# A hybrid RWKV-7 and delta-net layer on one core: delta-net decays from broadcast rows of running sums, 32x32 tiles in the heads' inversion, and a new order

## The chip, the cores and the metric

The kernel runs on one core of one Trainium2 chip. The metric is the device time of one execution in microseconds (us). Three runs of the kernel before took 2287.71 to 2296.7 us, median 2291.92 us.

## The reference, cut to what matters

One layer over 256 latent tokens and 256 context tokens, model width 2048, all float32. A projection `w_in` feeds two mixers: a bidirectional RWKV-7 mixer (16 heads of 64) and a bidirectional gated delta-net (8 heads of 128). Their outputs are merged under gates, projected, and a SwiGLU network follows. What the change touches is the delta-net's decay. Per head, direction and chunk of tokens, with g the log-decay of a token:

```
gc = jnp.cumsum(chunks(g), axis=-1)
diff = gc[..., :, None] - gc[..., None, :]
decay = jnp.where(incl, jnp.exp(jnp.where(incl, diff, 0.0)), 0.0)
lmat = jnp.where(strict, jnp.einsum('nbhik,nbhjk->nbhij', kb, kc) * decay, 0.0)
sol = lax.linalg.triangular_solve(lmat, rhs, left_side=True, lower=True, unit_diagonal=True)
qk = jnp.where(incl, jnp.einsum('nbhik,nbhjk->nbhij', qc, kc) * decay, 0.0)
q_dec = qc * jnp.exp(gc)[..., None]
```

The reference uses chunks of 64; the kernel works in blocks of 128 tokens, two latent and two context.

## The kernel before, in words

**Stages.** First come the modulation vectors and the low-rank columns (to about 300 us). Then one long woven stage holds the products with `w_in` and both mixers: eight RWKV pairs (to about 840 us), then eight delta-net heads (840 to about 1290 us). After it come the merge with `pa` and `pb`, `w_out`, the SwiGLU and the output (to 2289 us). Every large product splits float32 weights into a high part (`whi`, cast on ScalarE) and a low part (`wlo`, subtracted on VectorE) and runs three matmuls for each 128x128 tile of weights, into the PSUM tile `mm`.

**What sets the order.** The woven stage is written as generators (`prepare`, `grams`, `inverse`, `scan` per RWKV pair; `features`, `tokens`, `decays`, `head_grams`, `head_inverse`, `head_scan` per delta-net head; `products` and `cast` for the weights; `ada_rest` for the remaining modulation columns). A planner, `Weave`, gives each operation an estimated cost, picks the one that can start first, and breaks ties by a number per kind in `RANK`. The order that comes out is fixed on TensorE (PE), VectorE (DVE), ScalarE (ACT) and GpSimd (POOL), each of which runs its instructions in that order. DMAs that SyncE (SP) issues go in an order that the framework's scheduler sets. `GATES_A` and `GATES_B` say after which pair or head how many of the 40 gate products (fillers with no reader in this stage) become available.

**Decays.** For head h and direction d, `decays(h)` multiplies the column of log-decays by a triangle on DVE (tile `gm`, 128x512), multiplies that on PE by the constant matrix `aft[d]` (128x128 by 512 columns) to get all differences of running sums, takes Exp out of PSUM on ACT into `Ed{d}`, and masks it with the triangle on POOL. A second matmul, of `ones` by the first 256 columns of `gm`, gives the running sum itself, the same on every partition; ACT takes Exp of it into `eq`, and DVE multiplies q by it into `Qe`. `decays(h)` may begin when `head_grams(h-1)` is done; `head_grams(h)` reads `Ed0` and `Ed1`.

**Inversion.** `invert` solves the triangular systems: blocks of 16 go through DRAM (`scr`, `tscr`) and a loop of 15 steps on DVE, and are then joined into 32 and 64 by small matmuls into the PSUM tile `pi`. The RWKV pairs call it with nu=16, the heads with nu=8. In the joining step named in the diff, `Tx` is multiplied by `Qm` in 64x64 tiles, 16 matmuls of 16 columns for nu=8. Head h+1's inversion begins with the transposes `T<-LT` on DVE and the stores `scr<-LT` and `scr<-T` on SP.

**Names in the trace.** Nearly all planned instructions show the one line that records them (L146; L124 and L163 for the DMAs of POOL and SP). Tiles in the shared arena read as `arena`, the constants as `C`, PSUM banks as `pa`, `pi`, `s`, `mm`. So `pa<-arena,C` of 128x512 on PE is the `aft` matmul, or the sum of squares of k in `features`; of 128x256 it is the `ones` matmul, or the sum of squares of q; `arena<-C,gtok` on DVE is the product `gm`; `arena<-arena,C` on POOL is the mask.

Of the kernel before, what the change touches and what calls it, by code (L numbers as in the profile page):

```python
# [11 lines left out]
F32 = mybir.dt.float32  # L12
# [15 lines left out]
GATES_A, GATES_B = (6, 2, 3, 4, 0, 1, 4, 3), (2, 3, 0, 1, 1, 0, 9, 1)  # L28

RANK = dict(cast=-94, lowrank=-64, prepare=53, grams=-6, inverse=-58, values=6, scan=-54, begin=181, head_scan=90, head_inverse=100, head_grams=123, decays=122, tokens=90, features=160, gate_out=137, lowrank_out=99, row_tile=486)  # L30
# [8 lines left out]
for _name, _w in (("ident", 128), ("ones", 128), ("bd64", 128), ("rmask", 256),  # L39
                  ("low16", 2), ("eye16", 32), ("tri", 256), ("aft", 256), ("q4", 4), ("q2", 2),  # L40
                  ("eps", 1), ("gneps", 1)):
    _C[_name] = (_n, _n + _w)
    _n += _w
# [12 lines left out]
def const_array():  # L56
    c = np.zeros((P, NC_COLS), np.float32)

    def put(name, a):
        lo, hi = _C[name]  # L60
        c[:, lo:hi] = np.asarray(a, np.float32).reshape(P, hi - lo)

    i = np.arange(P)
    put("ident", np.eye(P))
    put("ones", np.ones((P, P)))
    put("bd64", (i[:, None] // 64) == (i[None] // 64))
    s, t = (i % 64)[:, None], np.arange(64)[None]
# [8 lines left out]
    put("aft", np.concatenate([u > v, u < v], 1))  # L76
    put("q4", (i[:, None] % 4) == np.arange(4)[None])
# [34 lines left out]
class Lane:  # L112
# [5 lines left out]
    def __getattr__(self, name):  # L118

        def op(out, *a, **k):  # L120
            if name == "preload_act_table_set":
                return Op(self, 1.3, lambda: self.engine.preload_act_table_set(out))
            if name == "dma_start":
                return Op(self, 0.6 if self.each > 0.002 else 0.06, lambda: self.engine.dma_start(out, *a))  # L124
# [153 lines left out]
def emit(ctx: ExitStack, tc, A, out, dbg=None):  # L278
# [7 lines left out]
    g = Lane(G, 0.06, 0.0024, LAT["own"])  # L286
# [29 lines left out]
    aft = c_("aft").rearrange("p (d t) -> p d t", d=2)  # L316
    eps, gneps = c_("eps"), c_("gneps")
# [245 lines left out]
    def invert(pool, Lt, parts, nu, which, full, fill):  # L563
# [63 lines left out]
        yield [e.matmul(pv[64 * h:64 * h + 64, 1, u], Tx[64 * h:64 * h + 64, u, :], Qm[64 * h:64 * h + 64, u, :],  # L627
                        start=True, stop=True) for u in range(nu) for h in range(2)]
# [46 lines left out]
    btok = cst.tile([P, 4, 16], F32, name="btok")  # L675
    egc = cst.tile([P, 4, 16], F32, name="egc")
# [385 lines left out]
    def products():  # L1062
# [24 lines left out]
        while todo or nxt:  # L1087
# [27 lines left out]
            else:  # L1115
# [5 lines left out]
    gplaces = (("kvq", 1280, 2), ("l2s", 512, 1), ("gm", 512, 1), ("Ed0", 512, 1), ("Ed1", 512, 1), ("eq", T, 1), ("ob", 8 * T, 1),  # L1121
# [5 lines left out]
             "VX0": [P, 8, 2, 64], "VX1": [P, 8, 2, 64], "KB": [P, 2, 8, 2, 64], "ivx": [P, 16, 64], "Y": [P, 4, 64], "R1": [P, 2, 64],  # L1127
# [29 lines left out]
    def begin():  # L1157
# [6 lines left out]
        t2 = gs.tile([P, 512], F32, tag="gm", name="t2")[:, 0:P]  # L1164
# [18 lines left out]
        yield v.tensor_scalar(sp, sp, al, -1.0, ALU.mult, ALU.mult)  # L1183
        ps = yield pab
        yield [e.transpose(ps[:, 0:P], sp, ident), e.transpose(ps[:, P:2 * P], bet, ident)]
        yield v.tensor_copy(gtok, ps[:, 0:P].rearrange("p (b c) -> p b c", b=4)[:, :, 0:16])
        yield v.tensor_copy(btok, ps[:, P:2 * P].rearrange("p (b c) -> p b c", b=4)[:, :, 16:32])
# [92 lines left out]
    def decays(h):  # L1280
# [6 lines left out]
        qe = []  # L1287
        for d in range(2):
            col = 8 * d + h
            gm = gs.tile([P, 4, P], F32, tag="gm", name="gm")  # L1290
            yield v.tensor_mul(gm, tri[:, d].unsqueeze(1).to_broadcast([P, 4, P]),
                               gtok[:, :, col:col + 1].to_broadcast([P, 4, P]))
            gf = gm.rearrange("p b c -> p (b c)")
            ps = yield pab
            yield e.matmul(ps, aft[:, d], gf, start=True, stop=True)
            ed = gs.tile([P, 4, P], F32, tag=f"Ed{d}", name="Ed")
            yield s.activation(ed.rearrange("p b c -> p (b c)"), ps, AF.Exp)
            weave.release(pab)
            yield g.tensor_mul(ed, ed, tri[:, d].unsqueeze(1).to_broadcast([P, 4, P]))
            Ed.append(ed)  # L1300
            if d == 0:
                yield "feat", h
                yield "scan", NPAIR - 1 if h else NPAIR - 2
                if h > 1:
                    yield "gscan", h - 2
                o["Qe"] = gs.tile([P, 2, T], F32, tag="Qe", name="Qe")
# [458 lines left out]
```

## Time and profile before

| what | value |
|---|---|
| median of three runs | 2291.92 us |
| the profiled execution's own time | 2291.02 us |
| its span, first to last instruction | 2289.2 us |
| granted TensorE clock, mean | 0.978 |
| busy share of the span: PE, DVE, ACT, POOL | 96%, 68%, 47%, 5% |

The 1.8 us between the profiled time and its span lie outside the instructions. PE's busy time counts pipelined matmuls whose ends are modelled; the distance from one start to the next says what a matmul really costs. `PEld` is the weight load that goes with each matmul.

### The profile page before, as it was taken

What the parts mean: (1) busy time and instruction counts of PE and PEld (TensorE: products, weight loads), DVE (VectorE), ACT (ScalarE), POOL (GpSimd) and SP (SyncE); (2) the same over time, 40 slices, a digit from 0 to 9 for tenths busy, and PEclk for the clock granted to TensorE, in tenths of its full rate; (3) what the DMA queues carried; (4) which work ended last, traced back from release to release, by engine and by line L of the source; (5) the groups of instructions that cost most, each with busy time, mean ns of one, the idle gap of its engine ahead of it and who ended that gap; (6) DMA issues with size and microseconds to landing.
All of it is one profiled execution on the core that took longest, in us unless ns stands there. A gap on an engine that the chain in (4) does not pass through costs nothing. (4 is left out here: it accounts for less than half of the span.)

```text
span 2289.2 us, 53997 instructions
## 1 busy us (share of the span) xinstructions
PE 2191.2 (96%) x22584; PEld 1944.7 (85%) x22584; DVE 1566.3 (68%) x3233; ACT 1068.0 (47%) x1894; POOL 115.2 (5%) x185
## 2 busy tenths in 40 slices
PE   7998999999999999999999989899999999999998
PEld 4766587777878778878889888889999999999997
DVE  3446488778888668888899768774656655545444
ACT  3245555444454455444545464443444444444443
POOL 0000000000000010111101040000000000000000
PEclk9999999989999999999999999999999999999999
DMA  9955544344343436455557777854777776566665
GB/s 388 402 143 166 171 119 131 94 104 108 107 118 107 119 106 190 142 165 157 166 160 251 250 280 266 290 194 144 233 240 235 235 231 213 188 184 192 187 188 162
DMA packets 231924, 430.72 MB, mean 188 GB/s; under 512 B 114944, under 2 KB 129152, under 8 KB 227328
## 3 DMA queue, kind: packets, MB, share of 16 engines
q1 hardware_dynamic: 203744, 350.72, 49.9%
q0 software_dynamic: 14112, 51.39, 7.1%
q10 hardware_dynamic: 13824, 25.17, 3.3%
q8 instruction: 177, 2.90, 0.5%
q14 instruction: 67, 0.55, 0.1%
HBM read 401.44 MB, written 25.77 MB: 187 GB/s over the span
## 5 line engine op out<-in xcount | busy, mean ns | idle before, releaser
L368 DVE TENSOR_TENSOR wlo<-wraw,whi 128x1024 fp32r<-128x1024 f32 x328 | 394.1, 1202 | 329.9 <-ACT whi L367 327.0
L367 ACT CAST whi<-wraw 128x1024 fp32r<-128x1024 f32 x328 | 337.6, 1030 | 478.9 <-PE mm L378 429.2
L146 PE MATMUL mm<-hxh,whi 128*128 128x256 f32 (+1 forms) x1376 | 467.5, 340 | 6.2 <-ACT whi L146 6.0
L146 PE MATMUL mm<-hxh,wlo 128*128 128x256 f32 (+1 forms) x1376 | 465.9, 339 | 4.1 <-DVE wlo L146 3.9
L146 PE MATMUL mm<-hxl,whi 128*128 128x256 f32 (+1 forms) x1376 | 465.7, 338 | 0.0
L379 PE MATMUL mm<-hfh,wlo 128*128 128x256 f32 x1344 | 376.1, 280 | 0.5 <-DVE wlo L368 0.5
L377 PE MATMUL mm<-hfh,whi 128*128 128x256 f32 x1344 | 376.1, 280 | 0.0
L378 PE MATMUL mm<-hfl,whi 128*128 128x256 f32 x1344 | 375.9, 280 | 0.0
L146 PEld LDWEIGHTS mm<-hxh,whi 128*128 128x128 f32 x1376 | 264.3, 192 | 33.9 <-ACT whi L146 7.4
L146 PEld LDWEIGHTS mm<-hxh,wlo 128*128 128x128 f32 x1376 | 264.2, 192 | 31.4 <-DVE wlo L146 6.1
L146 PEld LDWEIGHTS mm<-hxl,whi 128*128 128x128 f32 x1376 | 264.0, 192 | 25.9 <-issue 5.4
L146 DVE TENSOR_TENSOR wlo<-wraw,whi 128x512 fp32r<-128x512 f32 x344 | 236.5, 689 | 68.1 <-ACT whi L146 66.3
L146 ACT CAST whi<-wraw 128x512 fp32r<-128x512 f32 x344 | 205.0, 617 | 112.6 <-PE mm L146 79.0
L379 PEld LDWEIGHTS mm<-hfh,wlo 128*128 128x128 f32 x1344 | 253.2, 188 | 0.9 <-DVE wlo L368 0.9
L377 PEld LDWEIGHTS mm<-hfh,whi 128*128 128x128 f32 x1344 | 253.4, 189 | 0.0
L378 PEld LDWEIGHTS mm<-hfl,whi 128*128 128x128 f32 x1344 | 253.2, 188 | 0.0
L146 DVE TENSOR_TENSOR arena<-arena 128x28 f32<-128x28 f32 (+13 forms) x538 | 133.1, 249 | 23.6 <-DMA arena<-scr 10.5
L377 PE MATMUL mm<-za,whi 128*128 128x256 f32 x512 | 143.3, 280 | 0.0
L379 PE MATMUL mm<-za,wlo 128*128 128x256 f32 x512 | 143.2, 280 | 0.0
L378 PE MATMUL mm<-za,whi 128*128 128x256 f32 x512 | 143.2, 280 | 0.0
L378 PEld LDWEIGHTS mm<-za,whi 128*128 128x128 f32 x512 | 96.4, 188 | 0.0
L379 PEld LDWEIGHTS mm<-za,wlo 128*128 128x128 f32 x512 | 96.4, 188 | 0.0
(320 smaller groups left out, 3978.5 us busy)
## 6 DMA issues: line engine op xcount, KB each, us to landing
wraw<-w SPq DMA_DIRECT2D x172, 512.0 KB, 4.1
wraw<-wgu SPq DMA_DIRECT2D x168, 512.0 KB, 4.4
aw<-ada_rest POOLq DMA_DIRECT2D x96, 512.0 KB, 5.2
aw<-ada_first SPq DMA_DIRECT2D x32, 1024.0 KB, 11.2
wraw<-wdn SPq DMA_DIRECT2D x64, 448.0 KB, 3.7
wraw<-wout SPq DMA_DIRECT2D x32, 512.0 KB, 4.8
aw<-ada_gt ACTq DMA_DIRECT2D x64, 256.0 KB, 4.8
wraw<-wdn SPq DMA_DIRECT2D x32, 512.0 KB, 3.7
```

Source lines behind the costliest of these rows:

```text
L146: return Op(self, cost, lambda: getattr(self.engine, name)(out, *a, **k), kind)
L367: S.copy(hi[:, c, :M], raw[:, c, :M])
L368: V.tensor_sub(lo[:, c, :M], raw[:, c, :M], hi[:, c, :M].bitcast(F32))
L377: E.matmul(ps, hi, Xh[:, k, :n], start=first and i == 0, stop=False)
L378: E.matmul(ps, hi, Xl[:, k, :n], start=False, stop=False)
L379: E.matmul(ps, lo, Xh[:, k, :n], start=False, stop=last and i == len(wt) - 1)
```

## The change

Four things change together.

1. `begin` makes the running sums once: after the log-decays `sp` it adds two scans of 128x128 on DVE (forward and backward), stores their rows to a DRAM tile `grow` with eight small DMAs, and transposes them on PE along with the two transposes that were there, so that `gct` holds the sums by token.
2. `decays` has no matmul left. Per direction, one DMA reads a row of 512 sums from `grow` into all 128 partitions (`row`, one buffer); POOL subtracts `gct` from it; DVE takes the minimum with a new constant `past` (0 inside the triangle, -200 outside); ACT takes Exp. The Exp for `Qe` reads `row` itself, into `eq` for d=0 and in place for d=1. The wait for `features`, the scan and `gscan` moves behind both directions.
3. For nu=8 the step of `invert` becomes 32 matmuls in 32x32 tiles instead of 16 in 64x64.
4. Numbers that set the order: eight entries of `RANK`, `GATES_B`, and, in the planner, its two cost figures for POOL and the threshold by which it knows a DMA issued on POOL. The constants grow by 256 columns for `past`.

```diff
-GATES_A, GATES_B = (6, 2, 3, 4, 0, 1, 4, 3), (2, 3, 0, 1, 1, 0, 9, 1)
+GATES_A, GATES_B = (6, 2, 3, 4, 0, 1, 4, 3), (2, 2, 0, 1, 0, 1, 10, 1)
...
-    g = Lane(G, 0.06, 0.0024, LAT["own"])
+    g = Lane(G, 0.17, 0.0019, LAT["own"])
...
+        if nu == 16:
+            yield [e.matmul(pv[64 * h:64 * h + 64, 1, u], Tx[64 * h:64 * h + 64, u, :], Qm[64 * h:64 * h + 64, u, :],
+                            start=True, stop=True) for u in range(nu) for h in range(2)]
+        else:
+            yield [e.matmul(pv[r, 1, u], Tx[r, u, b:b + 32], Qm[r, u, :], start=True, stop=True) for h, u, b, r in fours]
...
+        yield v.tensor_tensor_scan(t0, ones, sp, 0.0, ALU.mult, ALU.add)
+        yield v.tensor_tensor_scan(t1[:, ::-1], ones, sp[:, ::-1], 0.0, ALU.mult, ALU.add)
+        for d, t in enumerate((t0, t1)):
+            for b in range(4):
+                dq(grow[d, :, P * b:P * b + P], t[32 * b:32 * b + 16])
...
-            gm = gs.tile([P, 4, P], F32, tag="gm", name="gm")
-            yield v.tensor_mul(gm, tri[:, d].unsqueeze(1).to_broadcast([P, 4, P]),
-                               gtok[:, :, col:col + 1].to_broadcast([P, 4, P]))
-            gf = gm.rearrange("p b c -> p (b c)")
-            ps = yield pab
-            yield e.matmul(ps, aft[:, d], gf, start=True, stop=True)
+            row = gs.tile([P, 4, P], F32, tag="row", name="row")
+            yield dq(row.rearrange("p b t -> p (b t)"), grow[d, 8 * d + h, :].partition_broadcast(P))
             ed = gs.tile([P, 4, P], F32, tag=f"Ed{d}", name="Ed")
-            yield s.activation(ed.rearrange("p b c -> p (b c)"), ps, AF.Exp)
-            weave.release(pab)
-            yield g.tensor_mul(ed, ed, tri[:, d].unsqueeze(1).to_broadcast([P, 4, P]))
+            yield g.tensor_sub(ed, row, gct[:, :, col:col + 1].to_broadcast([P, 4, P]))
+            yield v.tensor_tensor(ed, ed, past[:, d].unsqueeze(1).to_broadcast([P, 4, P]), ALU.min)
+            yield s.activation(ed.rearrange("p b c -> p (b c)"), ed.rearrange("p b c -> p (b c)"), AF.Exp)
             Ed.append(ed)
             if d == 0:
...
-            ps = yield pab
-            yield e.matmul(ps[:, :T], ones, gf[:, 0:T], start=True, stop=True)
-            eq = gs.tile([P, T], F32, tag="eq", name="eq")
-            yield s.activation(eq, ps[:, :T], AF.Exp)
-            weave.release(pab)
-            yield v.tensor_mul(o["Qe"][:, d], o["q"], eq)
+                first = gs.tile([P, T], F32, tag="eq", name="eq")
+                yield s.activation(first, row[:, 0:2].rearrange("p b c -> p (b c)"), AF.Exp)
+        yield "feat", h
+        yield "scan", NPAIR - 1 if h else NPAIR - 2
+        if h > 1:
+            yield "gscan", h - 2
+        o["Qe"] = gs.tile([P, 2, T], F32, tag="Qe", name="Qe")
+        yield v.tensor_mul(o["Qe"][:, 0], o["q"], first)
+        eq = row[:, 0:2].rearrange("p b c -> p (b c)")
+        yield s.activation(eq, eq, AF.Exp)
+        yield v.tensor_mul(o["Qe"][:, 1], o["q"], eq)
```

Over the whole program PE loses 16 matmuls of 128x512 and 16 of 128x256 and 128 of 64x16, and gains 256 of 32x16 and two transposes; DVE trades 16 products for 16 minima and gains two scans and two small copies; ACT's 32 Exps read SBUF instead of PSUM; POOL trades 16 products for 16 subtractions; SP gains 16 row loads and eight small stores.

PE in the middle of the delta-net stage, where the matmuls of one head's `w_in` columns (`mm`) run between the two steps `s<-TF,keg` that open a head's scan. Before:

```order
L146 MATMUL s<-TF_10240,keg 128x128 x4
L146 MATMUL mm<-hxh,wlo 128x512
L146 MATMUL mm<-hxh,whi 128x256
L146 MATMUL pa<-arena,C 128x512
L146 MATMUL s<-TF_10240,keg 128x128 x4
L146 MATMUL mm<-hxl,whi 128x256
```

The same step of a head after the change:

```order
L147 MATMUL mm<-hxl,whi 128x512
L147 MATMUL s<-TF_10136,keg 128x128 x4
L147 MATMUL mm<-hxh,wlo 128x512
L147 MATMUL mm<-hxh,whi 128x512
L147 MATMUL mm<-hxl,whi 128x512
L147 MATMUL mm<-hxh,wlo 128x512
L147 MATMUL mm<-hxh,whi 128x512
L147 MATMUL mm<-hxl,whi 128x512
L147 MATMUL s<-TF_10136,keg 128x128 x4
```

The decay's `aft` matmul is gone from between them; products alone fill the place.

DVE where one head's grams end (`PT`) and the next head's decay and inversion begin (`T<-LT`), with what each row waits for. Before:

```order
L146 TENSOR_TENSOR PT<-pa,arena 128x256
L146 SCALAR_TENSOR_TENSOR aw<-aw,ck 128x512 [waits DMASW4_49,DVE_49]
L146 TENSOR_TENSOR wlo<-wraw,whi 128x512 [waits DMAHW7_49,PE_49,Activation_49]
L146 TENSOR_TENSOR PT<-pa,arena 128x256
L146 SCALAR_TENSOR_TENSOR aw<-aw,ck 128x512 [waits DVE_49]
L146 TENSOR_TENSOR wlo<-wraw,whi 128x512 [waits Activation_49]
L146 COPY arena<-pi 128x256 [waits PE_49]
L146 TENSOR_TENSOR arena<-C,gtok 128x512
L146 SCALAR_TENSOR_TENSOR aw<-aw,ck 128x512 [waits DMASW5_49,DVE_49]
L146 SCALAR_TENSOR_TENSOR aw<-aw,ck 128x512 [waits DVE_49]
L146 STREAM_TRANSPOSE T_12267<-LT 64x256
```

After, the stretch from the minimum of direction 0 to the minimum of direction 1 (`arena<-arena,C`) of one head:

```order
L147 TENSOR_TENSOR arena<-arena,C 128x512 [waits Pool_49]
L147 SCALAR_TENSOR_TENSOR aw<-aw,ck 128x512 [waits DMASW3_49,DVE_49]
L147 SCALAR_TENSOR_TENSOR aw<-aw,ck 128x512 [waits DVE_49]
L147 STREAM_TRANSPOSE T_11582<-LT 64x256
L147 SCALAR_TENSOR_TENSOR aw<-aw,ck 128x512 [waits DMASW4_49,DVE_49]
L147 STREAM_TRANSPOSE T_11582<-LT 64x256
L147 TENSOR_TENSOR wlo<-wraw,whi 128x512 [waits DMAHW1_49,PE_49,Activation_49]
L147 SCALAR_TENSOR_TENSOR arena<-mm,PR,arena 128x2x254 [waits Activation_49]
L147 SCALAR_TENSOR_TENSOR aw<-aw,ck 128x512 [waits DVE_49]
L147 TENSOR_TENSOR wlo<-wraw,whi 128x512 [waits Activation_49]
L147 SCALAR_TENSOR_TENSOR arena<-mm,PR,arena 128x2x255 [waits DVE_49]
L147 TENSOR_TENSOR arena<-arena,C 128x512 [waits Pool_49]
```

The product that waited for nothing has become a minimum that waits for POOL, and ten rows stand between the two minima.

SP at the same head's start, with waits. Before, the stores that open an inversion:

```order
L163 DMA wraw<-w 128x1024 [waits DMAHW5_49,DVE_49]
L163 DMA scr_105<-LT 64x4x64 [waits DMAHW6_49,DVE_49]
L163 DMA scr_105<-LT 64x4x64 [waits DMAHW7_49]
L163 DMA wraw<-w 128x1024 [waits DMAHW2_49,DMAHW0_49,DVE_49]
L163 DMA scr_105<-T_12908 64x4x64 [waits DMAHW1_49,DVE_49]
L163 DMA scr_105<-T_12908 64x4x64 [waits DVE_49]
```

After:

```order
L164 DMA wraw<-w 128x1024 [waits DMAHW3_49,DVE_49]
L164 DMA scr_105<-LT 64x4x64 [waits DMAHW4_49,DVE_49]
L164 DMA scr_105<-LT 64x4x64 [waits DMAHW5_49]
L164 DMA wraw<-w 128x1024 [waits DMAHW6_49,DMAHW0_49,DVE_49]
L164 DMA arena<-grow 128x512 [waits DMAHW7_49,Activation_49,Pool_49]
L164 DMA scr_105<-T_11582 64x4x64 [waits DVE_49]
L164 DMA scr_105<-T_11582 64x4x64 [waits DMAHW1_49,DVE_49]
L164 DMA wraw<-w 128x1024 [waits DMAHW2_49,DVE_49]
```

The row load of direction 1, which waits for ACT and POOL, stands ahead of the stores `scr<-T`.

More of the change, by code (lines that the diff above doesn't have):

```diff
@@ L27 @@
 DECAY = 0.6065306597126334
-GATES_A, GATES_B = (6, 2, 3, 4, 0, 1, 4, 3), (2, 3, 0, 1, 1, 0, 9, 1)
-RANK = dict(cast=-94, lowrank=-64, prepare=53, grams=-6, inverse=-58, values=6, scan=-54, begin=181, head_scan=90, head_inverse=100, head_grams=123, decays=122, tokens=90, features=160, gate_out=137, lowrank_out=99, row_tile=486)
+GATES_A, GATES_B = (6, 2, 3, 4, 0, 1, 4, 3), (2, 2, 0, 1, 0, 1, 10, 1)
+RANK = dict(cast=-94, lowrank=-64, prepare=59, grams=-6, inverse=-56, values=6, scan=-39, begin=181, head_scan=145, head_inverse=100, head_grams=123, decays=122, tokens=77, features=120, gate_out=137, lowrank_out=105, row_tile=486)
 LAT = dict(dma=2.04, hop=0.255, own=0.092, grp=32, cg=4, turn=0.17)
@@ L39 @@
 for _name, _w in (("ident", 128), ("ones", 128), ("bd64", 128), ("rmask", 256),
-                  ("low16", 2), ("eye16", 32), ("tri", 256), ("aft", 256), ("q4", 4), ("q2", 2),
+                  ("low16", 2), ("eye16", 32), ("tri", 256), ("aft", 256), ("past", 256), ("q4", 4), ("q2", 2),
                   ("eps", 1), ("gneps", 1)):
@@ L123, in op @@
             if name == "dma_start":
-                return Op(self, 0.6 if self.each > 0.002 else 0.06, lambda: self.engine.dma_start(out, *a))
+                return Op(self, 0.6 if self.each > 0.0012 else 0.06, lambda: self.engine.dma_start(out, *a))
             n = int(np.prod(out.shape[1:]))
@@ L316, in emit @@
     aft = c_("aft").rearrange("p (d t) -> p d t", d=2)
+    past = c_("past").rearrange("p (d t) -> p d t", d=2)
     eps, gneps = c_("eps"), c_("gneps")
@@ L675, in emit @@
     btok = cst.tile([P, 4, 16], F32, name="btok")
+    gct = cst.tile([P, 4, 16], F32, name="gct")
+    grow = dpool.tile([2, 16, 512], F32, name="grow")
     egc = cst.tile([P, 4, 16], F32, name="egc")
```

24 lines of the change are left out of this document (10 added, 14 removed).

## The prediction, made before the changed kernel ran

> **What bounds the kernel now.** I read the busy times by stage first, then what PE waits for inside the stage that changes, then the rows around the matmuls that go. Busy time by stage; the columns are the stage and its length, PE, PEld, DVE, ACT, POOL, the granted clock, the DMA share and GB/s:
>
> ```profile
> 300.00:840.00 540.00, 525.07 (x7500) 425.35 (x7499) 426.90 (x1053) 276.15 (x639) 16.77 (x42) 0.97 0.41 108
> 840.00:1290.00 450.00, 438.68 (x4246) 377.51 (x4246) 388.55 (x1012) 218.46 (x433) 51.73 (x76) 1.00 0.60 177
> 1290.00:1560.00 270.00, 244.88 (x2060) 235.21 (x2060) 197.75 (x287) 131.61 (x204) 41.85 (x53) 0.95 0.73 251
> 1560.00:2260.00 700.00, 699.48 (x5993) 699.07 (x5992) 385.72 (x502) 303.78 (x374) 0.00 (x0) 1.00 0.68 209
> ```
>
> Delta-net heads run from 840 to 1290 us: PE is busy 438.7 of 450 us, idle 11.3. DVE is second with 388.6, so 61 us are left on it. All that PE waited for there (total, times, longest):
>
> ```profile
> PE pa L146 <- ACT arena L146: 6.0, 7, 1.3
> PE pi L146 <- DVE T L146: 2.7, 2, 1.7
> PE pi L146 <- DVE arena L146: 1.1, 3, 0.6
> PE s L146 <- DVE Vn L146: 0.6, 2, 0.3
> ```
>
> No wait for weights (`whi`, `wlo`) is among them, and none for the decays' products: the 6.0 us stand before the sum of squares in `features`. So **PE's own queue bounds this stage**, and a matmul taken out of it should shorten it by its length, until DVE or a DMA round trip is late instead.
>
> **What goes from PE.** Rows of PE in order of time (start, duration) around an `aft` matmul and a `ones` matmul:
>
> ```profile
> 1169.71 0.28 PE L146 MATMUL mm<-hxh,wlo 128*128 128x256 f32 x1
> 1169.83 1.02 PE L146 MATMUL pa<-arena,C 128*128 128x512 f32 x2
> 1170.29 0.68 PE L146 MATMUL mm<-hxh,whi 128*128 128x256 f32 x1
> 1170.81 0.28 PE L146 MATMUL mm<-hxl,whi 128*128 128x256 f32 x1
> ...
> 1173.19 0.28 PE L146 MATMUL mm<-hxh,wlo 128*128 128x256 f32 x1
> 1173.30 0.59 PE L146 MATMUL pa<-arena,C 128*128 128x256 f32 x2
> 1173.55 0.47 PE L146 MATMUL mm<-hxh,whi 128*128 128x256 f32 x1
> 1173.85 0.28 PE L146 MATMUL mm<-hxl,whi 128*128 128x256 f32 x1
> ```
>
> Products start 0.12 apart (1169.71 to 1169.83). From 1169.71 to 1170.81 are two such steps and the `aft` matmul: 1.10 - 0.24 = 0.86 us. From 1173.19 to 1173.85: 0.66 - 0.24 = 0.42 us. Each happens 16 times: **13.8 and 6.7 us**.
>
> The inversion's step, old form and a burst of the form that replaces it:
>
> ```profile
> 1236.13 1.11 PE L146 MATMUL pi<-arena,Tx 64*64 64x16 f32 x32
> 1237.17 0.39 PE L146 MATMUL mm<-hxh,whi 128*128 128x256 f32 x1
> ```
> ```profile
> 1171.72 0.73 PE L146 MATMUL pi<-T,LT 32*32 32x16 f32 x64
> 1172.37 0.39 PE L146 MATMUL mm<-hxh,wlo 128*128 128x256 f32 x1
> ```
>
> Start to start 1.04 against 0.65 us: 0.39 less, eight times, **3.1 us**. The new burst has the same count of tiles as the other 32x16 step, so I take its time. Two transposes are added:
>
> ```profile
> L146 PE MATMUL pa<-C,arena 128*128 128x128 f32 x226 | 36.2, 277 | 3.8 <-DVE LAc L146 2.9 <-DVE LAl L146 0.9
> ```
>
> 36.2 / 226 = 0.16 each, 0.3 together. PE's queue loses 13.8 + 6.7 + 3.1 - 0.3 = 23.3 us.
>
> **What the other engines trade.** Rows of DVE, POOL and ACT (busy, mean ns):
>
> ```profile
> L146 DVE TENSOR_TENSOR arena<-C,gtok 128x512 f32<-128x512 f32 x16 | 10.7, 672 | 0.0
> L146 DVE TENSOR_TENSOR arena<-arena 128x512 f32<-128x512 f32 x48 | 33.2, 702 | 0.7 <-POOL bon L826 0.3
> ```
> ```profile
> L146 POOL TENSOR_TENSOR arena<-arena,C 128x512 f32<-128x512 f32 x16 | 20.0, 1251 | 237.2 <-ACT arena L146 237.2
> ```
> ```profile
> L146 ACT ACTIVATE arena<-pa 128x512 f32<-128x512 f32 x16 | 9.6, 598 | 12.8 <-PE pa L146 12.8
> L146 ACT ACTIVATE arena<-arena 128x512 f32<-128x512 f32 x56 | 34.2, 629 | 14.5 <-issue 9.6 <-DVE arena L146 4.3
> L146 ACT ACTIVATE arena<-arena 128x256 f32<-128x256 f32 x32 | 13.3, 417 | 14.3 <-DVE arena L146 13.9
> ```
>
> DVE gives up 16 products of 0.67 us and takes 16 minima of the same shape (0.70 by the second row): half a microsecond in all. ACT's Exps differ by some 0.03 us each, POOL's subtraction has the mask's shape and count. DVE's and ACT's spare time hides all this; without cover it would be 16 x (0.03 + 0.06), 1.4 us. The scans, copies and eight stores of `begin` follow its transposes (`gtok`), 79 us ahead of the first grams (`LT`):
>
> ```profile
> 762.51 0.23 DVE L146 COPY gtok<-pa 128x64 f32<-128x64 f32 x1
> ...
> 841.87 0.87 DVE L146 SCALAR_TENSOR_TENSOR LT<-pa,nbtok,arena 128x128 f32<-128x128 f32 x3
> ```
>
> They cost nothing beside RWKV work, and what SP takes to issue them and the 16 rows delays weight loads for which PE never waited. The constants are 128 KB longer, and the start is bound by DMA:
>
> ```profile
> GB/s 388 402 143 166 171 119 131 94 104 108 107 118 107 119 106 190 142 165 157 166 160 251 250 280 266 290 194 144 233 240 235 235 231 213 188 184 192 187 188 162
> ```
>
> 131,072 B at 388 GB/s are **0.3 us**.
>
> **The wait that comes.** There is one `row` buffer, so direction 1's load waits for direction 0's subtraction and for the Exp into `eq`, which on ACT stands behind Exp of `Ed0`, which waits for the minimum of direction 0. From the end of that minimum the path is Exp 0.63, Exp 0.42, the load, subtraction 1.25, then the next minimum. No broadcast row is in the trace; the nearest loads (KB, median us to landing):
>
> ```profile
> arena<-sgd__1342 SPq DMA_DIRECT2D x32, 256.0 KB, 3.6
> ...
> arena<-oad SPq DMA_DIRECT2D x1, 1024.0 KB, 11.5
> ...
> T<-tscr SPq DMA_DIRECT2D x16, 64.0 KB, 2.4
> ...
> arena<-cvec SPq DMA_DIRECT2D x1, 1024.0 KB, 9.3
> ```
>
> Bounds are 2.4 and 11.5. I take 3.6, since `sgd` has this load's shape (128 rows of 2 KB), queue and size. The path is 0.63 + 0.42 + 3.6 + 1.25 = 5.9, and 6.4 with five handovers that I estimate at 0.1 each from this row (the `ones` matmul above ended at 1173.89, its Exp starts 0.05 later):
>
> ```profile
> 1173.94 0.38 ACT L146 ACTIVATE arena<-pa 128x256 f32<-128x256 f32 x1 [1.32 <-PE pa L146]
> ```
>
> The cover is what DVE has between the two minima, the ten rows shown in the change:
>
> ```profile
> L146 DVE SCALAR_TENSOR_TENSOR aw<-aw,ck 128x512 f32<-128x512 f32 x120 | 88.8, 751 | 5.9 <-DMA aw<-ada_rest 5.6
> ...
> L146 DVE STREAM_TRANSPOSE T<-LT 64x256 f32<-64x256 f32 x16 | 7.0, 435 | 0.2
> ```
> ```profile
> L146 DVE TENSOR_TENSOR wlo<-wraw,whi 128x512 fp32r<-128x512 f32 x344 | 236.5, 689 | 68.1 <-ACT whi L146 66.3
> ...
> L146 DVE SCALAR_TENSOR_TENSOR arena<-mm,PR,arena 128x510 f32<-128x510 f32 x32 | 23.6, 736 | 0.1
> ```
>
> Four times 0.75, two times 0.44, 0.69 and 0.74: 6.7 us. Cover and path are level, so I take half a microsecond per head for ACT's queue: **4.0 us**. At 2.4 us nothing is left of it; at 11.5 it is 14.3 - 6.7 = 7.6 per head, 61 us. Behind the waiting minimum on DVE stand `wlo` parts, for which products wait; behind the waiting load on SP stand `scr<-T`, which open the next inversion.
>
> The Trainium skill, DMA: Bandwidth & Descriptors, section Anatomy of one DMA — SWDGE (gpsimd) path, gives a DMA about 2.0 us fixed plus its bytes at 436 GB/s; for 256 KB an estimate by that page is 2.6 us. By it no wait would come, and the sum would be 4 us lower; `sgd`'s 3.6 us is longer than that, and the row is kept.
>
> **The order set anew** moves work among the 11.3 us of PE's idle time; at best it takes the 6.0 and 2.7 us above with it, at worst it adds as much. I take 0.
>
> **The sum**: 23.3 - 0.3 - 4.0 = 19.0 us. From the profiled execution's 2291.0 us (0.9 below the median of the three) this gives **2272 us**.
>
> **Rivals.** For the second one, 50 us of the stage:
>
> ```profile
> 1200.00:1250.00 50.00, 48.96 (x571) 45.85 (x570) 47.34 (x128) 27.87 (x57) 6.31 (x10) 1.00 0.74 225
> ```
>
> *Better* (14%): the load is early enough, and the waits of 6.0 and 2.7 us go too. 2272 - 4 - 9 = 2259. For it: `features` ranks earlier now. Against: the planner had these waits before, too.
> *DVE becomes the bound* (21%): its 388.6 us don't shrink. In a stage of 427 us it would be busy 91% of the time, against 86% now, in a fixed order in which each stall shows. If half of the 23.3 is lost to this, the time is 2280 to 2287, 2283 in the middle. For it: DVE has 2.7 of 50 us left in this row; against: PE waited for DVE 4.4 us in 450.
> *The change doesn't do what it says* (8%): PE was not the limit, and its time turns into waits on the heads' chain of inversions. Only the shorter inversion step is left, 2288. For it: PEld is busy 377.5 of 450 us; against: products start every 0.12 us with no gap. The Trainium skill, Perfetto Trace Analysis, section Identifying the Most-Contended Engine, says that matmul busy time is a bad measure, and that weight-load busy time is the one to use. By it PE has 72 us of room in this stage and the bound would lie elsewhere; the waits of 11 us in all speak against it here.
> *The row load holds up SP* (9%, slower): if a broadcast from DRAM lands as late as `cvec`, the one broadcast in the trace, in 9.3 us, the path is 12.1, and DVE and the stores `scr<-T` wait 5.4 us per head, 43 us in eight heads. Less 23, this is 2291 + 20 = 2311. It turns the sign from a wait of 2.9 us per head (23.3 / 8), a landing of 6.7 us. For it: the path is a loop in series through four queues. Against: `cvec` moves four times the bytes while the DMAs are 73% busy, here 60%. The Trainium skill, DMA: Bandwidth & Descriptors, in the same section, says that a wait is served on the issuing sequencer before dispatch, so that all behind it waits; SP's order makes that matter here.
>
> **How the numbers follow.** My forecast has 48%. The range runs from the better rival, 2259, to 2293, past the rivals without effect; the slower one is left out with 9%, and about as much in tails. A measurement of this kernel can tell about 0.5%, 11.5 us, from no change. Faster by more than that (below 2280.5) takes the forecast, the better rival and a third of the DVE rival: 48 + 14 + 7 = 69%. Within it are the rest of that one and the 8%: 22%. Slower: 9%.
>
> **What would show it.** Right: the head stage ends about 19 us sooner, PE has no `pa<-arena,C` but those of `features`, and PE idle stays under 17 us in it. The load lands in 3 to 4.5 us; DVE's minima wait for POOL under 1 us each. Wrong: DVE waits for POOL of several us before each second minimum, or SP waits before `arena<-grow` with `scr<-T` late; PE waits on `pi` or `wlo` that grow by 10 us or more.

## The result, and the profile after

The changed kernel takes 2268.36 us (median of 11 runs, 2259.78 to 2280.95), the kernel before beside it 2287.64 us (median of 11, 2280.68 to 2296.70). The ratio is 0.9917, 95% interval 0.9894 to 0.9939, which is 14 to 24 us: 19.3 us between the medians, where the prediction had 19.0. The profiled execution took 2273.03 us, its span is 2271.0 us.

The size is right; the way to it is less so. First the stages, cut at the same work in both kernels: the first inversion bursts of RWKV pair 0, of head 0 and of head 7, the FFN's first product, the end. Of the kernel before, then of after (columns: the stretch and its length, PE, PEld, DVE, ACT, POOL, granted clock, DMA share, GB/s):

```profile
259.10:895.50 636.40, 619.18 (x8518) 503.42 (x8517) 501.98 (x1225) 326.00 (x736) 25.14 (x55) 0.97 0.43 115
895.50:1285.10 389.60, 380.87 (x3821) 328.07 (x3821) 338.34 (x892) 188.71 (x378) 43.68 (x64) 1.00 0.59 173
1285.10:1533.60 248.50, 221.10 (x1939) 211.10 (x1938) 187.65 (x263) 124.22 (x189) 42.38 (x54) 0.96 0.80 275
1533.60:2289.20 755.60, 744.24 (x6340) 743.18 (x6340) 411.50 (x546) 319.87 (x402) 0.00 (x0) 0.99 0.64 200
```
```profile
256.80:873.40 616.60, 603.65 (x8441) 489.16 (x8440) 491.12 (x1217) 322.50 (x728) 24.69 (x55) 0.98 0.42 118
873.40:1262.30 388.90, 371.23 (x4031) 323.39 (x4030) 344.22 (x903) 191.33 (x383) 43.38 (x64) 0.99 0.61 184
1262.30:1509.40 247.10, 222.07 (x1999) 212.81 (x1998) 189.82 (x265) 125.84 (x192) 38.93 (x54) 0.97 0.81 279
1509.40:2271.00 761.60, 750.75 (x6340) 749.89 (x6340) 411.55 (x546) 319.67 (x402) 0.00 (x0) 0.99 0.64 199
```

Head 0's inversion comes 22 us sooner (895.5 to 873.4), head 7's 23 us (1285.1 to 1262.3). So in these two executions the lead is there before the heads' first inversion, and between the first and the last of them nothing more is won: 389.6 against 388.9 us. Counted along PE's order with the start-to-start costs of the prediction, some 13 us less of matmuls stand ahead of head 0's inversion (first decays, and products that the new order puts later), some 13 us less between head 0's and head 7's, and 3 us of products more behind it. In the second stretch the 13 us did not become time: PE's idle time there grows from 8.7 us (389.60 - 380.87) to 17.7, and the time at half clock from 3.4 to 10.2 us, which costs 3 more. What PE waited for from 820 to 1270 us of after (total, times, longest):

```profile
PE pa L147 <- ACT arena L147: 6.7, 6, 1.7
PE s L147 <- DVE Vn L147: 4.6, 3, 3.2
PE mm L147 <- ACT whi L147: 1.3, 1, 1.3
PE pi L147 <- issue: 1.2, 1, 1.2
```

The wait of 6.0 before `features` (`pa`) is still there as 6.7, and one on a head's scan (`s<-Vn`, 0.6 before) has come. Behind it stands the wait that the prediction priced. DVE's minima and POOL's subtractions (busy, mean ns, idle time before them), the row loads beside the load from which their landing was taken (KB, median us), and the new burst of 32x32 tiles:

```profile
L147 DVE TENSOR_TENSOR arena<-arena,C 128x512 f32<-128x512 f32 x16 | 11.0, 685 | 8.8 <-POOL arena L147 8.8
L147 POOL TENSOR_TENSOR arena<-arena,gct 128x512 f32<-128x512 f32 x16 | 19.8, 1240 | 151.5 <-DMA arena<-grow 127.2 <-DVE PT L147 24.3
```
```profile
arena<-sgd__1344 SPq DMA_DIRECT2D x32, 256.0 KB, 3.3
...
arena<-grow SPq DMA_DIRECT2D x16, 256.0 KB, 4.0
```
```profile
1207.99 0.73 PE L147 MATMUL pi<-arena,Tx 32*32 32x16 f32 x64
1208.65 0.38 PE L147 MATMUL mm<-hxh,whi 128*128 128x256 f32 x1
```

Durations came out as taken: the minimum 0.685 us (taken 0.70), the subtraction 1.24 (1.25), the burst 0.66 (0.65). The row lands in 4.0 us (median) and not in 3.6, and DVE waits 8.8 us for POOL in eight heads where 4.0 was taken. The loop of one head, from the first minimum over the Exp that frees the row, the load and the subtraction to the second minimum:

```profile
997.10 0.69 DVE L147 TENSOR_TENSOR arena<-arena,C 128x512 f32<-128x512 f32 x1
999.63 0.42 ACT L147 ACTIVATE arena<-arena 128x256 f32<-128x256 f32 x1
1000.11 0.33 SPq L164 DMA_DIRECT2D arena<-grow  x1
1005.04 1.04 POOL L147 TENSOR_TENSOR arena<-arena,gct 128x512 f32<-128x512 f32 x1 [6.91 <-DMA arena<-grow]
1006.12 0.69 DVE L147 TENSOR_TENSOR arena<-arena,C 128x512 f32<-128x512 f32 x1 [1.70 <-POOL arena L147]
```

The load is issued 2.3 us after the end of the first minimum and takes 4.9 to land, and the second minimum starts 8.3 us after that end, 1.7 of them waiting.

In the FFN after lost 6 us (755.6 to 761.6) with the same 6340 matmuls. In 200 us of that stage PE ran 1717 matmuls before and 1701 after:

```profile
2000.00:2200.00 200.00, 200.00 (x1717) 200.00 (x1716) 98.57 (x103) 87.68 (x105) 0.00 (x0) 1.00 0.64 188
```
```profile
2000.00:2200.00 200.00, 200.00 (x1701) 200.00 (x1700) 98.53 (x104) 87.54 (x107) 0.00 (x0) 1.00 0.64 186
```

It is 1% with no clock, wait or DMA to show for it. Eleven of the twelve experiments' profiles have 1716 or 1717 in this stretch, one (e12) has 1701 too, and this execution was 4.7 us above its median, e12's 14.2 above its own. So it looks like a property of single executions and not of the kernel; the cause stays open.

### The profile page after: what moved, and what is told of

The parts are those of the page before. It is cut to its first block, busy times and chain, and to the rows that moved or that the text cites. A ratio compares the mean times of both kernels' runs of the same rounds, so it can differ in the third digit from the quotient of the medians.

```text
span 2271.0 us, 54427 instructions
## 1 busy us (share of the span) xinstructions
PE 2168.7 (95%) x22778; PEld 1931.1 (85%) x22778; DVE 1563.7 (69%) x3237; ACT 1068.6 (47%) x1894; POOL 111.0 (5%) x185
## 4 chain that ended last, share of the span: by engine, by line
PE 66%; DVE 9%; issue 8%; DMA 4%; ACT 2%; POOL 1%; SPq 0%; DVEq 0%; ACTq 0%; POOLq 0%
PE mm L147 17%; PE mm L381 12%; PE mm L380 12%; PE mm L379 12%; PE s L147 5%; PE pa L147 4%; DVE arena L147 3%; PE pi L147 2%; DMA wr<-wgu 1%; DVE wlo L147 1%; DMA aw<-ada_rest 1%; DVE wlo L370 1%; DVE aw L147 1%; ACT arena L147 1%; DVE acc L1540 0%
## 5 line engine op out<-in xcount | busy, mean ns | idle before, releaser
L147 ACT ACTIVATE arena<-arena 128x512 f32<-128x512 f32 (+3 forms) x132 | 76.7, 593 | 49.6 <-DVE arena L147 36.8
```

What stands on the lines that cost most here:

```text
L147: return Op(self, cost, lambda: getattr(self.engine, name)(out, *a, **k), kind)
```

## The experiments

Each ran beside the kernel before. The third and fourth columns split the mean time of a kernel's runs by the granted clock of each run: what is lost to the clock is taken as time x (1 - clock), since in all these traces every stretch that isn't at 1.00 is at 0.50, which costs half its length if PE has work in all of it, and the rest is what is left. The standard error of a mean of the rest is 0.6 to 1.8 us, so that a difference of two is good to some 2 us. Three sets of the kernel before have a rest of 2243.2, 2245.5 and 2245.0 and 41, 42 and 41 us lost.

| kernel | ratio to before, 95% interval | rest, us | lost to the clock, us |
|---|---|---|---|
| after | 0.9917 (0.9894 to 0.9939) | 2228.4 | 40 |
| e1, order alone | 0.9986 (0.9971 to 1.0001) | 2245.3 | 35 |
| e2, 32x32 list alone | 1.0023 (1.0002 to 1.0045) | 2241.7 | 46 |
| e3, after with the old order | 1.0043 (1.0024 to 1.0061) | 2235.2 | 57 |
| e4, decays alone | 0.9958 (0.9935 to 0.9981) | 2227.1 | 48 |
| e11, decays and list in e4's order | 0.9969 (0.9949 to 0.9990) | 2228.8 | 50 |
| e6, after with the old list, same order | 0.9911 (0.9886 to 0.9935) | 2227.3 | 39 |
| e7, 16 matmuls put back | 0.9958 (0.9940 to 0.9977) | 2240.4 | 38 |
| e9, rows loaded twice | 1.0061 (1.0037 to 1.0086) | 2243.5 | 56 |
| e5, two rows | 0.9983 (0.9962 to 1.0004) | 2236.5 | 46 |
| e10, first Exp early | 0.9897 (0.9878 to 0.9917) | 2221.9 | 40 |
| e8, gaps filled | 0.9908 (0.9877 to 0.9939) | 2231.3 | 34 |
| e12, gaps filled, later casts | 0.9890 (0.9869 to 0.9910) | 2231.5 | 31 |

### The parts of the change

**e1_order_alone**: the kernel before with the new numbers (seven entries of `RANK` differ, not eight).

```diff
-RANK = dict(cast=-94, lowrank=-64, prepare=53, ...
+RANK = dict(cast=-94, lowrank=-64, prepare=59, ...
-GATES_A, GATES_B = (6, 2, 3, 4, 0, 1, 4, 3), (2, 3, 0, 1, 1, 0, 9, 1)
+GATES_A, GATES_B = (6, 2, 3, 4, 0, 1, 4, 3), (2, 2, 0, 1, 0, 1, 10, 1)
```

> The kernel before with nothing but the new order: the new RANK and GATES_B, and the planner's two new costs for POOL. TensorE's work is that of before. Theory (the gain is TensorE's shorter queue, the order is worth nothing): within 5 us of before, ratio 0.998 to 1.002. Rival (the gain is the order's): 10 to 20 us faster, ratio 0.991 to 0.996. A third: these numbers were set for the new decays and misplace the old ones, so that the queue waits more: 5 to 20 us slower, ratio 1.002 to 1.009.

0.9986: with the old decays the new numbers are worth some 3 us, by the interval none to 7. The rest is 2 us longer, and 6 us less go to the clock.

**e2_tiles_alone**: the kernel before with the heads' list in 32x32 tiles.

```diff
+        if nu == 16:
...
+        else:
+            yield [e.matmul(pv[r, 1, u], Tx[r, u, b:b + 32], Qm[r, u, :], start=True, stop=True) for h, u, b, r in fours]
```

> The kernel before with nothing but the heads' inversion list in 32x32 tiles (eight lists, one for each head). Theory (TensorE's queue is the bound, and the bursts go from 1.04 to 0.65 us): 3.1 us faster, ratio 0.9986, which an interval of some 0.2% hardly tells from 1. Rival (the burst stands in a chain of waits that other engines set, so its length is hidden): 1.000.

1.0023: neither. The rest falls by 1.5 us, but 5 us more go to the clock. The edit isn't confined to its line: the planner takes another cost and kind for the list, and the order changes in all that comes behind.

**e3_old_order**: the kernel after with the old numbers (the diff of e1, reversed).

> The kernel after with the order undone: the old RANK, GATES_B and planner costs, with the new decays and the 32x32 list kept. Theory (TensorE loses 23.3 us of work, the new waits give 4 back, the order gives nothing): 19 us faster than before, ratio 0.9917, from 0.990 to 0.994. Rival (the order is what gains): 0.997 to 1.001. A third, half by half: 0.994 to 0.997.

1.0043, 29 us behind after (0.0126 of 2287), and no theory had that. By the split 17 us more are lost to the clock and the rest is 7 us longer (the two ran beside different sets of before). Where the heads end, the product with `pa` finds its weights not yet cast (waits of PE from 1290 to 1335 us; after has 0.9 us of this at its own place, from 1262 to 1330):

```profile
PE mm L379 <- ACT whi L369: 8.1, 2, 6.4
```

**e4_decays_alone**: after with the old numbers and the 64x64 list.

> The kernel before with the new decays alone: old order, old 64x64 list. Theory: 13.8 + 6.7 us of matmuls go, 0.3 us of transposes and 0.3 of constants come, new waits take 4: 16 us faster, ratio 0.993, from 0.991 to 0.995. Rival (VectorE bounds the heads' stage, so that at most half of the matmuls' time is gained): 0.996 to 0.998. Against e3_old_order, which has the 32x32 list as well, it shows again what the list is worth: 0.0014 by the theory.

0.9958, 10 us: between the theory's range (to 0.995) and the rival's (from 0.996), and the interval reaches into each. By the split the rest falls by 16.1 us (2243.2 to 2227.1), which is the theory's 16, and 7 us more than before go to the clock; so it takes no bound by DVE to halve the gain, but the times alone don't decide it. In this order DVE waits 3.0 us for POOL, with rows that land in 3.9 us:

```profile
L147 DVE TENSOR_TENSOR arena<-arena,C 128x512 f32<-128x512 f32 x16 | 10.9, 680 | 3.0 <-POOL arena L147 3.0
```

**e11_tiles_in_e4_order**: the 32x32 list in e4's order (the old numbers, and the planner told the old list's cost).

```diff
+            for o in last:
+                o.cost, o.kind = 0.5 * (0.01 + 0.00075 * 16), (64, 64)
```

> The new decays and the 32x32 list in the issue order of the decays alone (the planner is told the cost and kind of the 64x64 list): it differs from e4_decays_alone by the eight lists alone, and from e3_old_order by nothing but what the planner was told. Theory (e3_old_order is slow by its order, and not by the tiles): as e4_decays_alone or up to 3 us faster, ratio to before 0.994 to 0.997. Rival (the 32x32 list itself does harm when it stands in this order): as e3_old_order, 1.003 to 1.006.

0.9969, as e4. So the list does no harm, and e3 is slow by the order that the list's cost led the planner to: e3 and e11 run the same instructions, 0.0074 apart, with intervals that don't meet.

**e6_old_tiles_same_order**: after's order, with 64x64 tiles.

```diff
+            for o in last:
+                o.cost, o.kind = 2 * (0.01 + 0.00037 * 16), (32, 32)
```

> The kernel after with the heads' second inversion list again in 64x64 tiles, while the planner is told the cost and the kind of the 32x32 list: the issue order of all engines stays row for row. Theory (eight bursts of 1.04 in place of 0.65 us on a queue that is the bound): 3 us slower than after, ratio to before 0.993. Rival (the list hides in waits of the stage): as after, 0.9917. If the 32x32 list did harm by itself, as the kernel with it and the old order might suggest: 5 to 15 us faster than after, ratio 0.985 to 0.9895; if that harm came from the order that its cost led the planner to, none of it shows here.

0.9911 against 0.9917. At a fixed order the rest is longer with the new list than with the old one, by 1.1 us here (good to 2) and by 1.7 in e11 against e4 (good to 1.2), where 3.1 less was expected. The rival holds as far as this can tell: the burst is 0.38 us shorter, and no gain from it shows.

The same four runs show what the order is worth with the new decays. e4 and e6 run the same instructions, one in the order drawn with the old numbers and one in after's, and so do e11 and after. The ratio falls by 0.0047 and by 0.0052, 11 and 12 us; the rest is the same within 0.4 us in both pairs, and 9 and 10 us less are lost to the clock.

### Is PE's queue the limit?

**e7_matmuls_back**: two matmuls of constants for each head, ahead of the transposes of v and of k into the same bank, which overwrite them. The rest of the order is after's.

```diff
+            for _ in range(n):
+                E.matmul(ps, ident, C[:, 0:ps.shape[1]], start=True, stop=True)
```

> The kernel after with 16 matmuls of 128x512 of constants put back on TensorE, two for each head, each ahead of the transposes of the tokens into the bank that these overwrite; the planner is not told of them, so that the order of the rest stays. Theory (a matmul in the heads' queue costs its 0.86 us): 13.8 us slower than after, ratio to before 0.9977. Rival (they fall into TensorE's waits, some 19 us in this stage): within 4 us of after, 0.990 to 0.9935. A third, by the clock: work in a wait keeps TensorE from the half clock, so that they cost less than they last, or nothing.

They cost what they should on PE (start to start 0.85 us, 13.6 in all):

```profile
917.50 1.02 PE L570 MATMUL pa<-C 128*128 128x512 f32 x2
918.35 0.60 PE L147 MATMUL pa<-C,arena 128*128 128x128 f32 x4
```

The rest grows by 12.0 us (2228.4 to 2240.4), the lost clock falls by 2, and the ratio rises by 0.0041, 9 us. So most of a matmul's time on PE is time of the kernel here, and PE's queue is the limit; the little that is missing I put down to idle time that the matmuls fill. The 2 us of clock are inside the noise.

### What the new wait costs

**e9_row_twice**: each row is loaded twice.

```diff
+            Q.dma_start(row.rearrange("p b t -> p (b t)"), grow[d, 8 * d + h, :].partition_broadcast(P))
             yield dq(row.rearrange("p b t -> p (b t)"), grow[d, 8 * d + h, :].partition_broadcast(P))
```

> The kernel after with each of the 16 row loads issued twice, the second behind the first's landing, so that a row is there some 4 us later and SP's queue is held by that long; the order of all other rows stays. It prices the rival in which the row load holds up SP and VectorE. If the rows' landing is on the path as that rival had it (turning point 6.7 us, then each microsecond eight times): some 8 us a row, 15 to 40 us slower than after, ratio to before 0.998 to 1.009. Theory (cover by other work of 6.7 us; VectorE's wait grows by 3 to 4 us a head, and TensorE has other work for most of it): 3 to 10 us slower than after, 0.993 to 0.996. If all of it is hidden: 0.9917.

1.0061: 33 us behind after and 14 behind before. Each load lands in 3.8 us, so that the row is whole after some 7.6, past the 6.7 at which the prediction put the turning point. DVE's wait of one head, then the sum of them:

```profile
1081.49 0.48 DVE L147 SCALAR_TENSOR_TENSOR arena<-mm,PR,arena 128x255 f32<-128x255 f32 x1
1086.30 0.69 DVE L147 TENSOR_TENSOR arena<-arena,C 128x512 f32<-128x512 f32 x1 [4.33 <-POOL arena L147]
```
```profile
L147 DVE TENSOR_TENSOR arena<-arena,C 128x512 f32<-128x512 f32 x16 | 11.0, 685 | 36.4 <-POOL arena L147 36.4
```

DVE waits 27.6 us more than in after. The rest grows by 15 us, and 16 more go to the clock: by this split the added waits are paid about twice here.

**e5_two_rows**: a second row buffer (512 columns more); `eq` (256 columns) goes.

```diff
-... ("row", 512, 1), ("Ed0", 512, 1), ("Ed1", 512, 1), ("eq", T, 1), ("ob", 8 * T, 1),
+... ("row", 512, 2), ("Ed0", 512, 1), ("Ed1", 512, 1), ("ob", 8 * T, 1),
...
-                first = gs.tile([P, T], F32, tag="eq", name="eq")
+                first = row[:, 0:2].rearrange("p b c -> p (b c)")
```

> The kernel after with two row buffers: the Exp for Qe of direction 0 goes in place over its row instead of into eq, whose room the second row takes, so that the load for direction 1 no longer waits for that Exp. The order on VectorE, ScalarE and POOL is that of after, and on TensorE's up to the FFN. Theory (the wait of VectorE for direction 1's subtraction, 8.8 us in the run, is all or nearly all on the path): 4 to 9 us faster than after, ratio to before 0.988 to 0.990. Rival (TensorE has other work in that time): as after, 0.9917.

0.9983. DVE's wait for POOL is gone (0.6 us in the run), yet the kernel is slower than after. It doesn't answer the question, as this kernel no longer computes the layer: the second buffer shifts the tiles behind it in the arena by 512 or 256 columns, I take it onto places that other tiles still hold (not traced). Its waits are others, too: PE waits 6.3 us for `Vn` and 4.6 us for `St` at the last heads.

**e10_exp_early**: the Exp that holds the one row buffer goes ahead of Exp of `Ed0`; the planner isn't told.

```diff
+            if d == 0:
+                first = gs.tile([P, T], F32, tag="eq", name="eq")
+                early = s.activation(first, row[:, 0:2].rearrange("p b c -> p (b c)"), AF.Exp)
+                sub.call = lambda a=sub.call, b=early.call: (a(), b())[0]
+                early.call = lambda: None
```

> The kernel after with the Exp of direction 0's row for Qe issued on ScalarE beside POOL's subtraction, ahead of the Exp of Ed, so that the one row buffer comes free some 1.5 us sooner; the planner takes it to be where it was, so the order on TensorE (up to the FFN), VectorE and POOL stays. The wait of VectorE for POOL (8.8 us in the run of after) should fall to 0 to 3 us. Theory (that wait is half on the path): 2 to 6 us faster than after, ratio to before 0.989 to 0.991. Rival (TensorE has other work meanwhile): as after, 0.9917.

0.9897, inside the theory's range: 4.6 us below after by the ratio, 6.5 by the rest (good to 2), at the same lost clock. DVE's minima wait for POOL no more (0.6 us), and the heads' stage (head 0's burst at 870.3, head 7's at 1250.6) takes 380.3 us where after took 388.9; PE idles 13.9 us in it and not 17.7, and the 10.2 us at half clock of that execution of after have no counterpart here:

```profile
L147 DVE TENSOR_TENSOR arena<-arena,C 128x512 f32<-128x512 f32 x16 | 10.9, 679 | 0.6 <-POOL arena L147 0.6
```

So by the middle values half or more of the 8.8 us were on the path; between the theory's 4.4 and all of them the runs don't decide. The intervals of e10 and after overlap, so that the times alone don't exclude the rival; the vanished wait and the shorter stage speak against it.

### The clock

**e8_fill**: 16 matmuls of constants into idle time of PE, ahead of inversion lists of pairs 0, 2, 3 and 6.

```diff
+                                    {0: (0, 4), 2: (6, 0), 3: (0, 4), 6: (0, 2)}.get(p, (0, 0)))
```

> The kernel after with 16 matmuls of 128x256 of constants at four places of the RWKV pairs where TensorE stood idle for 0.8 to 2.9 us and then ran at half clock for 3.4 to 10.2 us: ahead of the inversion's second list in pairs 0 (4), 3 (4) and 6 (2), ahead of its first list in pair 2 (6). They are 6.9 us of matmuls at 0.43, laid into idle time; order and results are those of after. Theory (idle time of a microsecond or two brings the half clock that follows): most of the 27 us at half clock goes, 8 to 13 us faster than after, ratio to before 0.986 to 0.988. Rival (the small matmuls of the inversion bring the half clock, whatever stands before them): as after or up to 4 us slower, 0.9917 to 0.9935.

Pair 2 of after, rows of PE (start, duration, idle time before it) and windows, in which the last three columns are granted clock, DMA share and GB/s:

```profile
414.90 1.27 PE L147 MATMUL pi<-arena 32*32 32x16 f32 x111
419.08 0.32 PE L147 MATMUL pi<-arena 32*32 32x16 f32 x17 [2.91 <-issue]
421.81 2.43 PE L147 MATMUL pi<-arena,Tx 64*64 64x16 f32 x42
```
```profile
416.00:420.00 4.00, 1.09 (x39) 0.67 (x28) 1.25 (x5) 0.00 (x0) 0.00 (x0) 0.94 0.40 154
420.00:424.00 4.00, 4.00 (x47) 3.01 (x46) 1.21 (x2) 2.89 (x7) 0.00 (x0) 0.50 0.05 12
424.00:428.00 4.00, 4.00 (x35) 3.45 (x34) 2.47 (x9) 1.24 (x5) 0.00 (x0) 0.50 0.23 66
428.00:432.00 4.00, 4.00 (x75) 3.01 (x74) 2.80 (x5) 3.19 (x9) 0.00 (x0) 0.78 0.01 2
```

2.9 us of idle time, then 10.2 us at half clock. The same place in e8:

```profile
418.94 2.75 PE L570 MATMUL pi<-C 128*128 128x256 f32 x12
421.62 0.96 PE L147 MATMUL pi<-arena 32*32 32x16 f32 x92
```
```profile
420.00:424.00 4.00, 3.70 (x139) 2.77 (x138) 1.20 (x5) 0.00 (x0) 0.00 (x0) 1.00 0.32 123
424.00:428.00 4.00, 4.00 (x75) 3.42 (x76) 2.28 (x6) 2.89 (x7) 0.00 (x0) 1.00 0.07 18
```

All four stretches at half clock are gone from the profile (a new one has come at 352 us, behind 1.0 us idle). Over the runs it is less: 5.4 us fewer are lost, the rest is 3 us longer (perhaps by the fill), and 0.9908 can't be told from after. That idle time brings the half clock here stands, as the small matmuls that follow are the same in both: at this place of pair 2 each of the twelve profiles without the fill has a stretch at half clock, of 3.4 to 13.7 us, and neither of the two with it (e8, e12) has one. The expected 8 to 13 us did not come.

**e12_fill_and_later_casts**: e8, and the casts of the FFN's first weights later in ScalarE's order.

```diff
+            tc.keep_in_program_order(Q.dma_start(raw, src[:, k0:k0 + 8, :]))
+            yield
+            for i in range(0, 8, wstep[0]):
...
+                tc.keep_in_program_order(S.copy(hi[:, c], raw[:, c]))
```

> A try for a faster kernel: e8_fill, and the FFN's first gate weights (wr) cast two steps of the output product after their load is issued and not straight behind it, so that ScalarE doesn't stand 6.5 us before the casts that TensorE waits for (3.9 us of idle time at the first steps of that product, and 6.8 us at half clock behind it). Theory (idle time, and the half clock that it brings): 3.9 + 3.4 = 5 to 8 us faster than e8_fill, ratio to before 0.987 to 0.989. Rival (the wait only moves to the later steps): as e8_fill, 0.991.

PE's wait for casts in front of the output product, in e8 from 1275 to 1510 us and in e12 from 1280 to 1520 (total, times, longest; the lines of the program are shifted by 12):

```profile
PE mm L379 <- ACT whi L369: 6.2, 5, 3.9
```
```profile
PE mm L391 <- ACT whi L369: 4.4, 6, 1.6
```

The one wait of 3.9 us is gone; 0.9890 is 4 us better than e8, inside the intervals. e10 and e12 are the fastest of all kernels here; the two together were not run.

## Why the prediction came out right

The size was met in part by luck. The prediction's 19.0 us were 15.9 for the decays with their wait, 3.1 for the list and nothing for the order. At the old order the decays gave 10 us (e4), the list gave nothing that shows, and the order gave 11 to 12, all of it through the clock.

**The bound.** Right. e7 shows it: of 13.6 us of matmuls put back into the heads' stage 12 count in the rest, 9 in the time. The rival by which PE was not the limit falls with it; the weight loads' 323 of 389 us were no room.

**The decays, 13.8 + 6.7 less 0.6, less a wait.** Right in the rest (e4: 16.1 for 15.9, good to 1), although only 10 us came out in time, and in after the way there was another: the lead of 22 us stands ahead of head 0's inversion. 13 of it are matmuls that no longer lie ahead of it, 5 come from less half clock among the RWKV pairs (37 us at half clock before, 27 after, each costing half its length), 2 stood ahead of pair 0 already, and some 2 are unassigned. The 5 belong to the two executions shown: over all runs before and after lose the same to the clock. I had expected the lead to grow over the eight heads; PE's idle time there, which was to stay under 17 us, came to 17.7 and took most of the heads' share, and half clock the rest.

**The list, 3.1.** The step that failed is "0.39 less, eight times": the burst is 0.38 shorter on PE, but at fixed orders (after against e6, e11 against e4) the rest with it is 1 and 2 us longer, not 3.1 shorter. That its end sits in the inversion's chain is argued, not shown.

**The new wait, 4.0.** Mis-sized: 8.8 us of waiting on DVE (seven waits of 1.1 us on the mean from 820 to 1275 us, the longest 1.7), of which e10 gets 6.5 back in the rest; the sign that each would stay under 1 us failed, as four of them don't.

In the seven heads where DVE waited for the second minimum (8.2 us in all), that minimum started 7.3 us on the mean after the end of the first, where 6.9 was taken with the half microsecond for ACT's queue. The queue was priced well, as the loads are issued after 1.8 us (taken 1.85); the landings were not, at 4.3 us on the mean of these heads, the longest 5.4. And DVE reached the second minimum after 6.1 us and not 6.7, which was the cover of one head. The excess came with the order: with the same instructions DVE waits 3.0 us in e4 and 9.2 in e6, 3.0 in e11 and 8.8 in after, since in the old order it reaches the second minimum later (7.8 us after the first in e4, 6.5 in after, means of eight heads).

By the estimate of 2.6 us worked out from the Trainium skill, DMA: Bandwidth & Descriptors, section Anatomy of one DMA — SWDGE (gpsimd) path, no wait would have come; that section is about DMAs that GpSimd issues, and for these rows, which SP issues, the measured 4.0 us of the landing and 8.8 us of waiting stand against it.

**The order, 0.** Near for the numbers alone (e1, some 3 us), wrong for the kernel after: with the new decays the order is worth 11 to 12 us (e4 against e6, e11 against after), and none of it shows in the rest. The numbers can't be taken apart from the edit: with the old ones the changed kernel is slower than before (e3), because the planner redraws the whole order from the list's new cost. After's 0.9917 rests on numbers that were set for it.

**The rivals.** *Better* did not come: PE's wait before `features` went from 6.0 to 6.7. *DVE becomes the bound*: DVE is busy 344 of 389 us (88%), and its stalls do reach PE, but through the wait of the row and not for lack of time: in e10, without that wait, DVE has the same 344 us of work in a stage of 380. *The row load holds up SP* is real once the row is late: with 7.6 us to the whole row its own sum gives 8 x (6.4 - 3.6 + 7.6 - 6.7) = 30 us of waits against 23 gained, 6 us slower than before; e9 measured 14, and 36 us of waits. Of these waits some 15 us appear in the rest against after, and 16 more went to the clock, which the sum lacked. The turning point, which the prediction's own terms put at 6.8 and not 6.7, was not measured: e9 is one landing beyond it.

**The term that was missing.** Nothing in the prediction priced what idle time of PE does to the clock. It came out right since before and after lose the same 40 us. The same instructions lose 40, 50 and 57 us in three orders (after, e11, e3), which is nearly as much as the whole gain.

## What to carry to other kernels

Price the loop of a new round trip by its slow landings and not by the median alone, and read what stands between its ends for every use, in the order that will run: the same edit waited 3.0 us in one order and 8.8 in another. Then free the buffer as early as the data allow, which here was one Exp moved ahead (4.6 us by the ratio, 6.5 by the rest). Where a planner draws the order from costs, compare edits at a fixed order (tell the planner the old cost), or the redrawn order is what is measured. And watch the granted clock where TensorE idles: the long waits that e9 added cost as much again in the clock, while the short ones that e10 took away gave none back.

## What the runs showed of the hardware

In the profile of after, 14 stretches between 30 and 1520 us are at half clock, some 75 us in all, each 3.4, 6.8 or 10.2 us long, and each begins within 5 us of idle time of PE of 0.8 to 3.4 us. The reverse holds for long idle times alone: each of the ten of 1.85 us and more is followed by half clock, while 21 of those of 0.8 to 1.8 us are not (1.68 us up to 1070.97 and 1.80 up to 1348.58 among them, with the clock at 1.00 around both). What decides between the shorter ones stays open. One stretch in the heads' stage, where 1.7 us of idle time (4.00 - 2.30) stand in the window ahead:

```profile
1176.00:1180.00 4.00, 2.30 (x16) 1.77 (x14) 2.83 (x6) 3.95 (x5) 0.95 (x2) 1.00 0.68 166
1180.00:1184.00 4.00, 3.64 (x11) 2.54 (x12) 3.85 (x10) 2.39 (x5) 0.54 (x1) 0.58 0.78 260
```

The Trainium skill, TensorE: Matmul & The Clock Gate, Part 1: The HAM clock gate, says that the array goes to half its clock after at least one idle window of about 3.4 us, that the window is 3,413 ns long and runs freely. The lengths of 3.4 us and their multiples agree. The idle time differs: 2.91 us at 416, and single waits of 0.8 to 2.2 us elsewhere, stood ahead of half clock here, so that a window need not have been empty.
